# Attention with bias on one core: rests of q loaded earlier, moves of V placed later, a batch closed six outputs from the end, the last exp in two halves

## Chip, cores and metric

The kernel runs on one core of one Trainium2 chip. The metric is device time in microseconds (us) of one execution; lower is better. Five engines work side by side, each through its own list of instructions in order: PE (TensorE, matmuls; PEld is its weight load), ACT (ScalarE), DVE (VectorE), POOL (GpSimd) and SP (SyncE, which here only issues DMAs). Engines wait for one another through semaphores.

## The reference

```python
def reference(q, k, v, bias):            # q, k, v: (4, 8, 1024, 64) f32; bias: (1, 1, 1024, 1024)
    scale = 1.0 / np.sqrt(head_dim)
    scores = scale * np.matmul(q, k.transpose(0, 1, 3, 2))
    scores = scores + bias
    scores_max = np.max(scores, axis=-1, keepdims=True)
    attn = np.exp(scores - scores_max) / (np.sum(np.exp(scores - scores_max), axis=-1, keepdims=True) + 1e-8)
    return np.matmul(attn, v).astype(np.float32)
```

There are 32 heads of 1024 queries, 1024 keys and 64 features; one bias serves all heads.

## The kernel before

**Slots.** Heads come in 16 pairs, queries in 8 chunks of 128. One chunk of one head is a slot, so there are 256 slots. A slot goes through these steps:

- *Fill* (`fill`, L244; 8 matmuls of 128x128): PE writes the scores of 128 queries against 1024 keys into one of three places in PSUM, called 0, 1 and 2 (`places`). A place keeps the score sum of the slot that was there: operands of two neighbouring heads are stacked, one of them negated, so that a fill takes the old head's scores away as it adds the new head's, and the bias stays. A slot that starts a new chunk in a place writes the bias afresh first (L241, 8 more matmuls); slots 0 to 2, 42 to 44, 56, 70 to 72 and seven from 166 on do so. A fill must wait until the exp, or the first DVE step, of the slot that held its place is done.
- *Exp* (`exp`, L258): ACT reads the place and writes the exponentials as bf16, 128x1024 in one instruction. Twenty slots, all of place 2, go to DVE in its place ("DVE slots", `d_steps`): six instructions, of which the first (L275) copies the place out and so frees it, and the others (L280, L284, L287, L290, L295) work out the exponential from that copy, the last writing the bf16 result. No maximum is taken off: the scores are small.
- *Output* (`av`, L312; 8 matmuls): PE multiplies the exponentials with V, which carries a 65th column of ones for the row sum, into a PSUM tile that takes up to seven slots (a batch).
- *Evacuation* (`evac`, L320 and L322): when a batch is closed, DVE takes the reciprocal of the sums and multiplies; then one DMA for each run of neighbouring chunks stores to the output. These are issued on SP, those of the last batches on ACT's queue. The very last output has a tile of its own, `olast`.

**Operands.** K, Q, V and bias are loaded by DMAs that POOL issues in order (L138, L145, L155, L160, L165). K and Q of a pair are transposed on PE (`transposes`, L187 or L191), copied out on DVE (`copy_out`, L199, L201) and doubled into operands for the neighbouring pair (`double`, L210, L212; from pair 7 on by DMAs, L538, after a negated copy, L218). Pairs 0 and 1 load Q in two pieces: three chunks at the start, the other five ("rests", `qrest`) later; the first user of a rest is slot 42. V lands in one of two buffers and is copied by DVE into the wide array `vall` (`move_v`, L492); the load of V of pair p waits for the move of pair p-2.

**Order.** All engines' lists come from a planner written out in the kernel: it keeps an estimated clock for each engine, and always emits the step that could start first. On DVE it picks from `dve_q`, whose entries have an estimated ready time, a priority (0.3 for moves of V, 0.5 for the first step of a DVE slot, 1 for evacuations, 2 for work that is not urgent, 3 and 4 for the later DVE steps) and a cost. Which slots go to DVE is decided when they are filled, from the estimated amount of work that DVE has waiting (`backlog`, `ROOM`) and the number of DVE slots that are open (`open_d`, at most three). ACT takes, of the filled slots, the earliest. The estimates only set the order; on the chip each engine works through its list as the semaphores allow. The early loads are in an order written by hand; `issue` puts a later load on POOL behind a copy (`tick`, L467) that waits for the landing of the load before the last.

Of the kernel before, what the change touches and what calls it, by code (L numbers as in the profile page):

```python
# [16 lines left out]
def kernel(  # L17
# [30 lines left out]
    SPLIT, EARLY = 2, 7  # L48
# [40 lines left out]
    slots = []  # L89
# [20 lines left out]
    NS = len(slots)  # L110
# [10 lines left out]
        at_place[x[0]] = s  # L121

    dslots = set()
    may_d = [x[0] == 2 and 36 < s < NS - 18 and not any(y[3] for y in slots[s:s + 4]) for s, x in enumerate(slots)]

    raws, lands, arrs = {}, {}, {}

# [205 lines left out]
    with tc.manual_schedule():  # L335
# [65 lines left out]
        v_at, vland_at = {}, {0: 13000}  # L401
        t_dma = 15900
        DUE = (64, 82, 94, 106, 117, 126, 134, 142, 150)
        t_pe, t_act, t_dve, t_pool = 9300.0, 9900.0, 9600.0, 9000
        filled, used = {0: T0}, {0: 9900 + L_ACT}
        av_done = {}
# [18 lines left out]
        next_fill, next_act = 1, 1  # L425
        avq = list(range(NS))
        acts = [0]
        dav = []
        dve_q = []
# [7 lines left out]
        sp_q, t_sp = [], T0  # L437
        AHEAD, SLACK = 60, 300
        DEP = 115
        ROOM = 5000  # L440
        MARGIN = 0
        WINDOW = 4

# [46 lines left out]
        def move_v(pr):  # L490
            def run(t2):
                nc.vector.tensor_copy(vall[:, 2 * pr % VR:2 * pr % VR + 2, :, :D], lands[pr, "v"][:])  # L492
                v_at[pr] = t2 + 480 + L_DVE
                next_v(v_at[pr])
            dve_q.append((vland_at[pr], 0.3, 480, run))


        def early(kind, pr):
# [76 lines left out]
        def pe_cands():  # L575

            out = []
            for x in range(3):
                if not queue[x] or queue[x][0] > next_fill + WINDOW:
                    continue  # L580
                s = queue[x][0]
                r = fill_ready(s)
                if r is not None and (before[s] is None or before[s] in used):
                    cost = FILL + BIAS * bool(slots[s][3] and s > 1)

                    def do(t, s=s, x=x, cost=cost):
                        nonlocal next_fill
                        fill(s)
                        filled[s] = t + cost + L_PE
                        queue[x].pop(0)  # L590
                        next_fill = min([y[0] for y in queue.values() if y], default=NS)
                        if may_d[s] and backlog(t) < ROOM and len(open_d) < 3:
                            dslots.add(s)
                            avq.remove(s)
                            start_d(s)
                        else:
                            acts.append(s)
                    out.append((max(t_pe, r), cost, do, 0, s))


            todo = []
            if avq:
                group = [s for s in avq[:1] if round_of[s] == round_of[avq[0]]]
                have = [s for s in group if s in e_at]
                lag = len([s for s in avq[:NE] if s in e_at])
                if len(have) < len(group):
                    group = have if lag >= LAG and have[:1] == avq[:1] else []
                if avq[0] >= NS - 3:
                    group = [s for s in avq[:1] if s in e_at]
                if group and all(slots[s][2] // 2 in v_at for s in group):  # L610
                    todo.append((max(max(e_at[s], v_at[slots[s][2] // 2]) for s in group), group))
            if dav:
                todo.append((dav[0][0], [dav[0][1]]))
            if todo:
                r, group = min(todo)
                b = len(closed)
                if b_tag:
                    tag = b_tag[0]
                    group = group[:7 - len(bank[b][1])]
                else:  # L620
                    f, tag = min((x_free[y], y) for y in x_free)
                    r = max(r, f)
                cost = AVG * len(group) if len(group) > 1 else AV
                if r < 1e11:
                    def do(t, group=group, b=b, tag=tag, cost=cost):
                        b_tag[:] = [tag]
                        x_free[tag] = 1e12
                        av(group, b, tag)
                        for s in group:
                            if s in dslots:  # L630
                                dav.pop(0)
                            else:
                                avq.remove(s)
                            av_done[s] = t + cost
                        next_v(t)
                        n = len(bank[b][1])
                        if n == 7 or n == 6 and not (dav and dav[0][0] < t + cost + 600) or len(av_done) in (NS - 1, NS):
                            closed.append(b)
                            b_tag.clear()
                            close(b, tag, t + cost + L_PE)  # L640
                    out.append((max(t_pe, r), cost, do, 1, 0))
            if pieces:
                pr, which, c0, n = pieces[0]
                need = need_at[pr, which, c0]
                ring = pr + linked(pr) - RING
                lag = len([s for s in avq[:NE] if s in e_at])
                if ((pr, which, c0) in raw_at and next_fill >= need - AHEAD and (ring < 0 or last_slot[ring] < next_fill)
                        and (lag < 4 or need - next_fill < 8)):
                    f, tag = min((x_free[y], y) for y in x_free)
                    r = max(f, raw_at[pr, which, c0])  # L650
                    cost = n * TR + SWITCH * (pr < EARLY or which not in BESIDE)
                    urgent = need - next_fill < 12
                    if r < 1e11:
                        def do(t, pr=pr, which=which, c0=c0, n=n, tag=tag, cost=cost):
                            x_free[tag] = 1e12
                            pieces.pop(0)
                            px = transposes(pr, which, c0, n, tag)
                            if pr < EARLY and which == 0 and c0 == 0:
                                freed(pr, t)

                            def run(t2):
                                copy_out(pr, which, c0, n, px)
                                done = t2 + 60 * n + (180 if which else 300)
                                x_free[tag] = done + L_DVE
                                if which:
                                    ready["ko", pr] = done + L_DVE
                                else:
                                    ready["qo", pr, c0] = done + L_DVE
                                doubles(pr, which, c0, n, done, urgent)
                            dve_q.append((t + cost + L_PE, 0 if urgent else 2, 60 * n + (180 if which else 300), run))  # L670
                        out.append((max(t_pe, r), cost, do, 2 if next_fill < need - 9 else 0.5, 0))
            return out
# [18 lines left out]

        chains, d_wait, open_d = [], [], set()

        def backlog(t):
            x = max(0, t_dve - t) + sum(y[2] for y in dve_q if y[0] < t + 3000 and y[1] < 3)
            return x + sum(sum(y[0] for y in c) for c in chains) / 2 + sum(sum(y[0] for y in c[1:]) for r, s, c in d_wait) / 2

        def start_d(s):
            steps = d_steps(s)
            open_d.add(s)  # L700

            def first(t):
                steps[0][1]()
                used[s] = t + steps[0][0] + L_DVE
                d_wait.append((t + steps[0][0] + DEP, s, steps))
                next_chain(t)
            dve_q.append((filled[s], 0.5, steps[0][0], first))
# [46 lines left out]
            return min(ok + fills, key=lambda x: (x[0], x[3])) if ok + fills else None  # L754

        def dve_pick():
            can = [x for x in dve_q if x[1] < 4 or len(dav) < 2]
            if not can:
                return None
            best = min(can, key=lambda x: (max(x[0], t_dve), x[1]))  # L760
            start = max(best[0], t_dve)

            if best[1] >= 3:
                soon = [x for x in dve_q if x[1] < 3 and x[0] < start + 350]
                if soon:
                    best = min(soon, key=lambda x: (x[0], x[1]))
            return best

        move_v(0)
        for x in ("k3", "q3", "v1", "k4", "q4", "v2", "k5", "q5", "v3", "k6", "q6", "v4", "v5", "b3", "q0", "q1", "b4", "v6", "b5", "b6", "b7"):  # L770
            early(x[0], int(x[1]))
        while next_fill < NS or next_act < len(acts) or avq or dav or dve_q or sp_q:
            c = []
# [21 lines left out]
            t, who = min(c)  # L795
            if who == 0:
                s = acts[next_act]
                exp(s)
                t_act = t + EXP
                next_act += 1  # L800
                used[s] = e_at[s] = t_act + L_ACT
# [41 lines left out]
```

## Time and profile before

| | |
|---|---|
| median of 3 runs | 233.38 us (233.37 to 234.59) |
| the profiled execution's own time | 235.16 us |
| its span (first to last instruction) | 233.4 us |
| granted TensorE clock in it | 0.997 |
| exps on ACT (L258) | 237 instructions, mean 1089 ns of one |
| first DVE steps (L275) | 20, mean 1220 ns |
| moves of V (L492) | 16, median 423 ns |
| loads of the rests of q | 2 of 160 KB as they are stored, median 8.3 us from issue to landing |

An exp's duration includes the time that it waits in ACT's pipeline behind the one before, so the step from one start to the next is the better measure of a busy ACT. The idle time that the profile names stands before an instruction, with what ended it. Idle time of an engine costs something only where another engine comes to wait for it.

### The profile page before, as it was taken

Reading aid. Unit: us, or ns where it says so; the run is one execution under the profiler, and the core shown is the slowest. Engines: PE = TensorE matmul, PEld = TensorE weight load, DVE = VectorE, ACT = ScalarE, POOL = GpSimd, SP = SyncE. Lnnn points to the kernel's source line nnn. Section 1 sums busy time; section 2 is a strip of 40 time slices with the busy share of each in tenths; the row PEclk is TensorE's granted clock in tenths of the full one; section 3 lists DMA queues with packets and bytes.
Section 4 is the critical chain, followed back from the end, with each engine's and each line's share of the span. In section 5 each row is a group of like instructions: output and inputs, shape, how many; then the busy total and the mean of one; then the engine's idle time right before and its main releaser. Section 6 shows DMA issues by size and latency. Waiting matters only on the chain. (4 is left out here: it accounts for less than half of the span.)

```text
span 233.4 us, 10703 instructions
## 1 busy us (share of the span) xinstructions
PE 222.3 (95%) x4671; PEld 209.3 (90%) x4671; DVE 201.5 (86%) x296; ACT 221.1 (95%) x241; POOL 63.4 (27%) x99
## 2 busy tenths in 40 slices
PE   7989999899999999999999997999999999999992
PEld 2869999798999999999999997999999999999982
DVE  2576677599999998999999869999998999999972
ACT  3799999988999999999999998999999999999993
POOL 8943135055446555245352310000000000000000
PEclk9999999999999999999999999999999999999998
DMA  6999979959999899999999992111111111221212
GB/s 206 206 205 215 224 166 158 229 121 150 120 191 137 131 159 183 204 196 157 197 163 201 204 194 68 44 42 39 44 37 42 45 42 42 65 59 42 66 48 56
DMA packets 55646, 29.75 MB, mean 127 GB/s; under 512 B 31472, under 2 KB 51952, under 8 KB 55600
## 3 DMA queue, kind: packets, MB, share of 16 engines
q0 software_dynamic: 30336, 14.06, 48.7%
q1 hardware_dynamic: 24832, 14.40, 22.6%
q8 instruction: 36, 0.59, 1.1%
q10 hardware_dynamic: 432, 0.62, 0.8%
q14 instruction: 10, 0.08, 0.1%
HBM read 29.36 MB, written 8.39 MB: 162 GB/s over the span
## 5 line engine op out<-in xcount | busy, mean ns | idle before, releaser
L258 ACT ACTIVATE E<-pl 128x1024 bf16<-128x1024 f32 (+1 forms) x237 | 218.0, 1089 | 4.3 <-PE pl L244 3.9
L312 PE MATMUL po<-vall,E 128*128 128x65 bf16 x1888 | 93.6, 194 | 0.9 <-ACT E L258 0.9
L312 PEld LDWEIGHTS <-E 128*128 128x128 bf16 x1888 | 78.1, 98 | 1.9 <-ACT E L258 1.2
L244 PE MATMUL pl<-qo,ko 128*128 128x128 bf16 x1024 | 77.3, 219 | 1.7 <-DVE dy L275 1.1
L244 PEld LDWEIGHTS <-ko 128*128 128x128 bf16 x1160 | 69.2, 98 | 4.5 <-issue 1.5
L244 PE MATMUL pl<-qe,ke 128*128 128x128 bf16 x888 | 66.8, 219 | 1.9 <-DVE qe L212 0.5
L244 PEld LDWEIGHTS <-ke 128*128 128x128 bf16 x888 | 53.2, 98 | 5.0 <-issue 1.3
L275 DVE TENSOR_SCALAR dy<-pl 128x1024 int32<-128x1024 f32 x20 | 24.4, 1220 | 2.1 <-PE pl L244 1.4
L322 DVE TENSOR_TENSOR ob<-po,rs 128x448 f32<-128x448 f32 (+2 forms) x39 | 23.2, 594 | 1.9 <-DVE rs L320 0.5
L295 DVE SCALAR_TENSOR_TENSOR de<-dy,dt 128x1024 uint16<-128x1024 int32 x20 | 24.4, 1218 | 0.0
L290 DVE SCALAR_TENSOR_TENSOR dt<-df,dt 128x1024 f32<-128x1024 f32 x20 | 24.4, 1218 | 0.0
L284 DVE SCALAR_TENSOR_TENSOR dt<-df 128x1024 f32<-128x1024 f32 x20 | 24.3, 1217 | 0.0
L287 DVE SCALAR_TENSOR_TENSOR df<-dt,df 128x1024 f32<-128x1024 f32 x20 | 24.3, 1216 | 0.0
L199 DVE COPY ko<-px 128x1024 bf16<-128x1024 bf16 (+1 forms) x16 | 10.7, 671 | 6.9 <-PE px L191 6.3
L165 POOL DMA_DIRECT2D v<-in_v_dram x16 | 11.4, 712 | 18.3 <-DVE vall L492 16.0
L138 POOL DMA_DIRECT2D q<-in_q_dram x18 | 16.0, 890 | 1.3 <-DMA out_dram<-ob 0.5
L201 DVE TENSOR_SCALAR qo<-px,sgn 128x1024 bf16<-128x1024 bf16 (+2 forms) x18 | 12.4, 688 | 4.4 <-PE px L191 3.6
L280 DVE TENSOR_SCALAR df<-dy 128x1024 f32<-128x1024 uint16 x20 | 13.8, 690 | 0.0
L241 PE MATMUL pl<-ident,braw 128*128 128x128 bf16 x136 | 11.5, 228 | 0.1
L145 POOL DMA_DIRECT2D k<-in_k_dram x15 | 11.0, 734 | 2.2 <-PE pl L244 1.0
L320 DVE RECIPROCAL rs<-po 128x7 f32<-128x7 f32 (+3 forms) x40 | 7.8, 195 | 4.4 <-PE po L312 4.0
L467 POOL COPY tick<-q 1x1 bf16<-1x1 bf16 x9 | 3.8, 421 | 24.7 <-DMA q<-in_q_dram 24.7
(54 smaller groups left out, 129.5 us busy)
## 6 DMA issues: line engine op xcount, KB each, us to landing
v<-in_v_dram POOLq DMA_DIRECT2D x16, 256.0 KB, 6.1
k<-in_k_dram POOLq DMA_DIRECT2D x15, 256.0 KB, 5.6
out_dram<-ob SPq DMA_DIRECT2D x32, 96.0 KB, 3.6
out_dram<-ob SPq DMA_DIRECT2D x45, 64.0 KB, 3.2
ke<-ko SPq DMA_DIRECT2D x22, 128.0 KB, 4.9
q<-in_q_dram POOLq DMA_DIRECT2D x18, 128.0 KB, 4.8
qe<-q SPq DMA_DIRECT2D x17, 128.0 KB, 4.9
out_dram<-ob SPq DMA_DIRECT2D x67, 32.0 KB, 1.8
```

The lines of the kernel that those rows point to most:

```text
L138: nc.gpsimd.dma_start(out=t[:, :, y, :], in_=(qf, kf)[x][pr][:, y].rearrange("p (c d) -> p c d", d=D))
L201: nc.vector.tensor_scalar(t["qo"][:, cs, :], px[:], sgn[:], None, op0=ALU.mult)
L244: nc.tensor.matmul(to, kk[:, kc, :], qq[:, c, :], start=False, stop=True, skip_group_check=True)
L258: nc.scalar.activation(e[:, i:i + n].rearrange("p b x -> p (b x)"), places[slots[s][0]][:, i:i + n].rearrange("p b x -> p (b x)"), ACTF.Ex ...
L275: w.tensor_scalar(t["y"][:], places[slots[s][0]].rearrange("p b x -> p (b x)"), scale * LOG2E * 65536.0, 127.0 * 65536.0, op0=ALU.mult, op ...
L280: w.tensor_scalar(t["f"][:], t["lo"], G / 65536.0, None, op0=ALU.mult)
L284: w.scalar_tensor_tensor(t["t"][:], t["f"][:], -G, t["f"][:], op0=ALU.add, op1=ALU.mult)
L287: w.scalar_tensor_tensor(t["f"][:], t["t"][:], Q, t["f"][:], op0=ALU.mult, op1=ALU.add)
L290: w.scalar_tensor_tensor(t["t"][:], t["f"][:], V, t["t"][:], op0=ALU.add, op1=ALU.mult)
L295: w.scalar_tensor_tensor(etile[s].bitcast(U16).rearrange("p c q -> p (c q)"), t["y"][:], 1.0 / 512.0, t["t"][:], op0=ALU.mult, op1=ALU.add)
L312: nc.tensor.matmul(po[:, j + i, :], etile[s][:, kc, :], vall[:, slots[s][2] % VR, kc, :], start=j + i + kc == 0, stop=kc == NCH - 1, skip_ ...
L322: nc.vector.tensor_tensor(ob[:, :n, :], po[:, :n, :D], rs[:, :n, :].to_broadcast([P, n, D]), op=ALU.mult)
```

## The change

The DVE slots are now a list (`PLAN`); it holds the same 20 slots that the rule chose before. Five edits act on the order:

- In the list of early loads, the rests of q of pairs 0 and 1 stand ahead of V of pair 5 and of the bias chunk 3.
- A move of V of pair 7 or later is taken as ready 1500 ns later than its estimated landing.
- A batch is also closed when 250 outputs are done.
- The last exp is issued as two instructions of 512 columns each; the output's matmuls on the first half wait for the first alone.
- A DVE slot counts as open from its first step, and the choice on DVE holds a first step back while three are open; before, the choice of DVE slots did so.

The lists of instructions that come out differ in many places after the early loads: DVE's from its 57th entry on, PE's from the first transpose of a rest on, and the order of the exps from slot 41 on, where the exps of place 2 come one or two later than before.

```diff
-    may_d = [x[0] == 2 and 36 < s < NS - 18 and not any(y[3] for y in slots[s:s + 4]) for s, x in enumerate(slots)]
+    PLAN = (38, 47, 50, 59, 75, 78, 96, 108, 117, 129, 150, 159, 171, 177, 189, 195, 207, 216, 225, 234)
...
-        ROOM = 5000
...
-            dve_q.append((vland_at[pr], 0.3, 480, run))
+            dve_q.append((vland_at[pr] + 1500 * (pr >= EARLY), 0.3, 480, run))
...
-                        if may_d[s] and backlog(t) < ROOM and len(open_d) < 3:
+                        if s in PLAN:
                             dslots.add(s)
                             avq.remove(s)
                             start_d(s)
...
-                        if n == 7 or n == 6 and not (dav and dav[0][0] < t + cost + 600) or len(av_done) in (NS - 1, NS):
+                        if n == 7 or n == 6 and not (dav and dav[0][0] < t + cost + 600) or len(av_done) in (NS - 6, NS - 1, NS):
...
         def start_d(s):
             steps = d_steps(s)
-            open_d.add(s)
-
             def first(t):
+                open_d.add(s)
                 steps[0][1]()
...
         def dve_pick():
-            can = [x for x in dve_q if x[1] < 4 or len(dav) < 2]
+
+            can = [x for x in dve_q if (x[1] < 4 or len(dav) < 2) and (x[1] != 0.5 or len(open_d) < 3)]
...
-                soon = [x for x in dve_q if x[1] < 3 and x[0] < start + 350]
+                soon = [x for x in can if x[1] < 3 and x[0] < start + 350]
...
-        for x in ("k3", "q3", "v1", "k4", "q4", "v2", "k5", "q5", "v3", "k6", "q6", "v4", "v5", "b3", "q0", "q1", "b4", "v6", "b5", "b6", "b7"):
+        for x in ("k3", "q3", "v1", "k4", "q4", "v2", "k5", "q5", "v3", "k6", "q6", "v4", "q0", "q1", "v5", "b3", "b4", "v6", "b5", "b6", "b7"):
...
-                exp(s)
+
+                for i in range(2) if next_act == len(acts) - 1 and next_fill >= NS else (None,):
+                    exp(s) if i is None else exp(s, i, 1)
```

More of the change, by code (lines that the diff above doesn't have):

```diff
@@ L692 @@
         chains, d_wait, open_d = [], [], set()
-        def backlog(t):
-            x = max(0, t_dve - t) + sum(y[2] for y in dve_q if y[0] < t + 3000 and y[1] < 3)
-            return x + sum(sum(y[0] for y in c) for c in chains) / 2 + sum(sum(y[0] for y in c[1:]) for r, s, c in d_wait) / 2
         def start_d(s):
             steps = d_steps(s)
-            open_d.add(s)
             def first(t):
+                open_d.add(s)
                 steps[0][1]()
```

## The prediction

> **What bounds the kernel now.** I read the busy table of the page first.
>
> ```profile
> PE 222.3 (95%) x4671; PEld 209.3 (90%) x4671; DVE 201.5 (86%) x296; ACT 221.1 (95%) x241; POOL 63.4 (27%) x99
> ```
>
> ACT, PE and DVE are all near full, so I ask what one exp costs when nothing holds it up. The chain of waits shows it at the end.
>
> ```profile
> 220.11 0.06 ACT E L258
> 220.17 0.84 issue
> ...
> 227.34 0.16 ACT E L258
> ```
>
> Eight exps start between 220.11 and 227.34: 7.23/8 = 0.904 us from one to the next, although one lasts 1.02 alone. The change keeps the same 20 slots on DVE and 236 on ACT, so that part cannot shrink; only time beyond 0.904 per exp can. The timeline of ACT (idle time before a row in brackets) shows where it is.
>
> ```profile
> 47.53 1.02 ACT L258 ACTIVATE E<-pl 128x1024 bf16<-128x1024 f32 x1 [0.26 <-PE pl L244]
> 48.76 1.02 ACT L258 ACTIVATE E<-pl 128x1024 bf16<-128x1024 f32 x1 [0.21 <-PE pl L244]
> 50.00 4.69 ACT L258 ACTIVATE E<-pl 128x1024 bf16<-128x1024 f32 x5 [0.21 <-PE pl L244]
> 55.28 1.02 ACT L258 ACTIVATE E<-pl 128x1024 bf16<-128x1024 f32 x1 [0.59 <-PE pl L244]
> ...
> 73.14 37.71 ACT L258 ACTIVATE E<-pl 128x1024 bf16<-128x1024 f32 x41 [0.34 <-PE pl L244]
> ...
> 143.24 17.56 ACT L258 ACTIVATE E<-pl 128x1024 bf16<-128x1024 f32 x19 [0.87 <-PE pl L244]
> ```
>
> ACT always waits for a fill. From the exp of slot 39 (44.38) to the last (228.25) there are 197 steps: 183.87 - 197 x 0.904 = 5.8 us lost. By stretch, each counted the same way: 44.38 to 58.91 (14 steps) 1.87; to 74.08 (16) 0.71; to 143.24 (74) 2.26, of which 1.03 in the last step; to 228.25 (93) 0.94. Next, what made PE late, from the timelines of PE and DVE:
>
> ```profile
> 42.11 0.47 PE L191 MATMUL px<-ident,qrest 128*64 128x128 bf16 x10 [0.78 <-DMA qrest<-in_q_dram]
> ...
> 142.59 0.61 PE L244 MATMUL pl<-qo,ko 128*128 128x128 bf16 x8 [1.14 <-DVE dy L275]
> ```
>
> ```profile
> 46.96 0.43 DVE L492 COPY vall<-v 128x1024 bf16<-128x1024 bf16 x1 [0.85 <-DMA v<-in_v_dram]
> ...
> 138.33 0.43 DVE L492 COPY vall<-v 128x1024 bf16<-128x1024 bf16 x1 [1.86 <-DMA v<-in_v_dram]
> ...
> 140.99 0.42 DVE L492 COPY vall<-v 128x1024 bf16<-128x1024 bf16 x1
> 141.32 1.22 DVE L275 TENSOR_SCALAR dy<-pl 128x1024 int32<-128x1024 f32 x1
> ```
>
> One PE stall is the late rest of q; the other is a first DVE step (L275, slot 150), which alone frees place 2, behind two moves of V. The tail, from the SP and ACT timelines:
>
> ```profile
> 225.81 5.35 SPq L688 DMA_DIRECT2D out_dram<-ob  x6
> ...
> 230.53 0.34 ACTq L688 DMA_DIRECT2D out_dram<-olast  x1
> ```
>
> The batch of seven evacuated at 228.91 gives SP five stores at 0.46 each; the last lands at 232.41, after olast (232.25). The span ends 0.98 later.
>
> **Part 1, rests of q ahead of V5.** Today POOL holds both rests behind V5's load, which waits for a V buffer until 32.77; they are issued at 34.05 and land at 42.07 and 43.32. Now they go out at about 27.9 with nothing to wait for, while the q0 queue is nearly empty from 32 to 34, so they land near 35 to 37, well before PE's transposes at about 41.8. No DMA is added. The PE stall goes and the exp of slot 39 starts near 43.9: **-0.48**.
>
> The new DVE order also puts the move of V6 ahead of the copy of q1's rest, its two doubles and slot 38's first step; before, only one double stood behind it. Added wait: DVE comes to it at about 43.5. Behind it on DVE stand 0.43 + 0.56 + 0.33 + 0.33 + 1.22 = 2.9 us to the end of the first step; for that waits PE's fill of slot 41, and behind that fill, in PE's order, all others. PE wants it at about 47.4, so V6 must land by 44.5. It landed at 46.94. Everything in its queue except the rests stays ahead of it; the rests took 42.07 - 38.38 and 43.32 - 42.07, together 4.94 us of the queue. I take that whole: V6 at 42.0, no wait. Ends: 42.0 and (nothing gained) 46.94; two rests at the second one's 1.25 give 44.4, still in time.
>
> The Trainium skill, page "DMA: Bandwidth & Descriptors", section "Anatomy of one DMA — SWDGE (gpsimd) path", fits a POOL-queue DMA as 2.0 us plus bytes over 436 GB/s. By it the two rests (2 x 327,680 bytes) hold the queue only 1.5 us, V6 lands at 45.4 and the sum below would be 0.9 worse. The 4.94 us of this trace speak for more.
>
> Between 44 and 59, what stays: slots 42 and 43 carry bias (16 matmuls, 1.13 us) and now run in two alternating places, since slot 41's comes later. A place that was freed at t gives data at t+1.13+0.05, with one exp (0.904) to cover it: 0.3 to 0.4 lost at each, 0.8 in all, and 0.2 at slot 54, whose fill stands behind slot 50's. So 1.0 for 1.87: **-0.87** (ends 0 and -1.87).
>
> **Part 2, slot order round the DVE slots.** A DVE slot now counts as open from its first step on, not from its fill; that acts only through the order, and the number of evacuations stays 40. The new order takes place 2's exp later, after a DVE slot. At slots 70 and 71 (bias fills, 0.61 lost in one step at 73.14) the order is now 70, 72, 71, so two exps cover each fill: **-0.6** (ends 0, -0.71).
>
> **Part 3, later moves of V.** Moves 7 to 15 stand later on DVE. V14's load waits for V12's move (two buffers) and landed 7.7 us after it; the DVE work between the two moves grows from 5.5 to 6.7 us, so its wait shrinks. Then slot 150's first step follows at once, where before a last step, a copy, a negate and V15's move (1.22+0.74+0.43+0.42 = 2.8) came between; and its successor's exp has one more exp of time. The 1.03 step goes: **-1.03** (ends 0, -1.03). On POOL, K11 and Q11 pass V7, K13 and Q13 pass V9; V9 then lands where Q13 did (106.6), DVE reaches its move near 108. No readers of these V come before it.
>
> **Small stalls.** The remaining 1.23 and 0.94 (alternating places, transposes between two fills) stay: exps that come only two after the last of their place go from 43 to 50. Ends -0.8, +0.8; I take 0.
>
> **Part 4, tail.** Let L be the start of the last exp: today olast is evacuated at L+2.25, the end is L+5.14. The new batch at six from the end takes the five SP stores off the end. But slot 234's last three steps move behind the small batch: its DVE chain starts when slot 248's output is there (L-3.2) and takes 0.75 + 1.14 + 0.55 + 1.14 + 1.22 = 4.8, to L+1.6. The last exp in halves: a half alone took 0.60, a whole 1.02, of which 0.12 hides behind the next one; two halves cost 0.06 to 0.09 more, and let four of eight output matmuls go early (4 x 0.033). So slot 255 is out at L+1.65. Then a batch of five (between 0.46 for two and 0.76 for six: 0.66) to L+2.36, two stores on ACT's queue at 0.42, slot 234 alone (0.43), its store third at L+3.2, landing 1.72 later as olast's did, and 0.98: L+5.9. **+0.8** (ends: 0 if ACT issues faster; +1.8 if DVE comes 1 us late).
>
> **Sum.** -0.48 - 0.87 - 0.6 - 1.03 + 0.8 = -2.2. The profiled execution took 235.16 with a span of 233.4, 1.8 around it; it becomes 233.0. The median of the three runs, 233.38, lies 1.8 below the profiled time; I move it by the same amount: **231.2**.
>
> **Rivals.** (a) *V6 late*: it lands at 45.4 to 46.9, DVE stands 2 to 3 us at the move, fill 41 blocks PE. Cost 0.9 to 2.4: 232.1 to 233.6. For it: DVE waited 0.85 there already. Against: the queue's idle time that the rests now fill. Chance 0.12. (b) *Stalls only move*: the 0.6 and the 1.03 turn up at other transposes and places since PE is nearly full; 232.8. For it: more alternating pairs. Against: DVE now has, up to slot 234's first step, 153.7 us of work against 182 exps, before 155.1 against 179. Chance 0.13. (c) *Slower*: first DVE steps come late. From the exp that frees place 2 to the next exp there: 1.10 + 0.61 + 1.22 + 0.05 + 0.61 + 0.1 = 3.7 us; eleven of the DVE slots leave five exps for it, 4.5 us. If a step of 1.22 already running holds DVE, and it comes over 0.8 late, the rest is lost at each; at 1.1 late on eleven that is 3.3, which makes it slower than before; at 1.22 late with an evacuation of 0.8 before it, 13 us. Against: before had five at nearly every slot and lost 0.94 in the last 85 us. 235.5 as a middle; chance 0.07. (d) *Small stalls go too*, and the tail costs nothing: 231.2 - 0.8 - 0.8 = 229.6; chance 0.1.
>
> **Numbers.** Forecast 0.58 (230.3 to 232.2). With (d), faster by over 0.5% (below 232.2) 0.67; (a), (b): within 0.5% 0.25; slower 0.08. 0.5% is about what a measurement of this kernel tells from no change. Range: from (d) to the dear end of (a), 229.6 to 233.7; out of it lie (c) and the far ends.
>
> **What would show it.** Right: no wait of PE for qrest; V6 landed before 44.5 and no DVE idle time at its move; the exp rows unbroken at 55, 73 and 143; last exp starting near 225.3; olast's store issued about 3.2 after it. Wrong: DVE waiting for v near 43 to 47 with a gap on PE at slot 41; new breaks of ACT over 0.5; a last DVE step after the last exp's end by more than 1 us.

## The result and the profile after

The changed kernel takes 234.93 us (median of 20 runs), the kernel before 233.68 us beside it: ratio 1.0044, 95% interval 1.0024 to 1.0064. It is slower by about 1.0 us; 231.2 was forecast, and 234.93 lies above the range.

The busy table of the changed kernel's page, one line: the engines do the same work as before.

```profile
PE 221.2 (95%) x4671; PEld 209.1 (90%) x4671; DVE 201.2 (86%) x296; ACT 221.0 (95%) x242; POOL 63.2 (27%) x99
```

The timeline of ACT of the changed kernel (start, length, group; in brackets the idle time before it), against the six rows shown of before:

```profile
45.18 1.98 ACT L257 ACTIVATE E<-pl 128x1024 bf16<-128x1024 f32 x2 [0.64 <-PE pl L243]
47.45 1.02 ACT L257 ACTIVATE E<-pl 128x1024 bf16<-128x1024 f32 x1 [0.29 <-PE pl L243]
48.68 25.04 ACT L257 ACTIVATE E<-pl 128x1024 bf16<-128x1024 f32 x27 [0.21 <-PE pl L243]
73.88 37.77 ACT L257 ACTIVATE E<-pl 128x1024 bf16<-128x1024 f32 x41 [0.17 <-PE pl L243]
111.83 116.81 ACT L257 ACTIVATE E<-pl 128x1024 bf16<-128x1024 f32 x128 [0.19 <-PE pl L243]
```

The breaks at 55 and 143 are gone, the one at 73 has shrunk from 0.34 to 0.17, and from 111.83 on ACT's 128 instructions are one row without a break that the timeline shows. What is new is the 0.64 ahead of 45.18: the exp of slot 39 comes 0.8 *later* than before (44.38), where it was to come 0.48 earlier. PE's timeline, and below it the weight loads, say why:

```profile
41.75 0.27 PE L243 MATMUL pl<-qe,ke 128*128 128x128 bf16 x2
42.93 0.49 PE L243 MATMUL pl<-qe,ke 128*128 128x128 bf16 x6 [0.91 <-issue]
43.35 0.47 PE L190 MATMUL px<-ident,qrest 128*64 128x128 bf16 x10
```
```profile
42.93 0.32 PEld L243 LDWEIGHTS <-ke 128*128 128x128 bf16 x5 [1.03 <-issue]
```

The transposes of the rest (L190) wait for no DMA any more: the rests landed at 34.0 and 35.3. But PE stands for a microsecond between the second and the third matmul of one fill, where no semaphore is in play; the profile can only call it "issue".

DVE, at the two places that the forecast named: the move of V6 (L490) and slot 38's first step (L274), then V14's move and slot 150's first step right behind it.

```profile
45.16 0.43 DVE L490 COPY vall<-v 128x1024 bf16<-128x1024 bf16 x1
...
46.80 1.22 DVE L274 TENSOR_SCALAR dy<-pl 128x1024 int32<-128x1024 f32 x1
...
140.48 0.42 DVE L490 COPY vall<-v 128x1024 bf16<-128x1024 bf16 x1
140.82 1.22 DVE L274 TENSOR_SCALAR dy<-pl 128x1024 int32<-128x1024 f32 x1
```

No row has idle time in front: V6 had landed at 44.0, V14 at 139.7. In the tail, from the timelines of DVE and ACT:

```profile
227.72 1.22 DVE L294 SCALAR_TENSOR_TENSOR de<-dy,dt 128x1024 uint16<-128x1024 int32 x1
...
229.87 0.22 DVE L321 TENSOR_TENSOR olast<-po,rs 128x64 f32<-128x64 f32 x1
```
```profile
229.79 0.83 ACTq L686 DMA_DIRECT2D out_dram<-ob  x2
230.72 0.39 ACTq L686 DMA_DIRECT2D out_dram<-olast  x1
```

Slot 234's last step ends after the last exp does (228.64). olast is evacuated at 230.09, but its store goes out only at 230.72, behind two other stores on ACT's queue. From the last exp's end to the end of the span it takes 4.55 (before: 3.84).

**The two profiles side by side mislead.** The spans are 233.19 and 233.39, so the changed kernel looks 0.2 *shorter*, while the medians say 1.25 longer. In every run here the time is the span and 1.8 more. Before's median of 233.68 thus belongs to a span of about 231.9, and the profiled execution of before was one of the longest of its kind. The experiments had to say which of its stalls were the kernel's and which that execution's.

### The profile page after: what moved, and what is told of

It is laid out like the page before. It is cut to its first block, busy times and chain, and to the rows that moved or that the text cites. A ratio compares the mean times of both kernels' runs of the same rounds, so it can differ in the third digit from the quotient of the medians.

```text
span 233.2 us, 10648 instructions
## 1 busy us (share of the span) xinstructions
PE 221.2 (95%) x4671; PEld 209.1 (90%) x4671; DVE 201.2 (86%) x296; ACT 221.0 (95%) x242; POOL 63.2 (27%) x99
## 4 chain that ended last, share of the span: by engine, by line
PE 45%; ACT 35%; issue 9%; DMA 4%; DVE 3%; POOL 3%; DVEq 0%; POOLq 0%
ACT E L257 35%; PE pl L243 26%; PE po L311 13%; DMA q<-in_q_dram 4%; PE px L190 3%; PE pl L240 2%; DVE dy L274 1%; POOL k L144 1%; PE px L186 1%; POOL braw L159 1%; DVE de L294 0%; DVE df L286 0%; DVE dt L289 0%; DVE ob L321 0%; POOL qz L349 0%
## 5 line engine op out<-in xcount | busy, mean ns | idle before, releaser
L311 PE MATMUL po<-vall,E 128*128 128x65 bf16 x1888 | 92.8, 194 | 0.2 <-ACT E L257 0.2
L311 PEld LDWEIGHTS <-E 128*128 128x128 bf16 x1888 | 77.8, 98 | 1.2 <-ACT E L257 0.5
L243 PEld LDWEIGHTS <-ko 128*128 128x128 bf16 x1160 | 69.9, 98 | 6.2 <-issue 2.7
L243 PEld LDWEIGHTS <-ke 128*128 128x128 bf16 x888 | 52.6, 98 | 4.1 <-issue 1.2
L274 DVE TENSOR_SCALAR dy<-pl 128x1024 int32<-128x1024 f32 x20 | 24.4, 1221 | 3.2 <-PE pl L243 3.0
L321 DVE TENSOR_TENSOR ob<-po,rs 128x448 f32<-128x448 f32 (+3 forms) x39 | 23.2, 594 | 1.9 <-DVE rs L319 0.2
L319 DVE RECIPROCAL rs<-po 128x7 f32<-128x7 f32 (+4 forms) x40 | 7.9, 197 | 4.8 <-PE po L311 3.9
L240 PEld LDWEIGHTS <-braw 128*128 128x128 bf16 x136 | 10.0, 148 | 0.1
```

The costliest lines, as they stand in the source:

```text
L240: nc.tensor.matmul(to, braw[:, c, :].rearrange("p (kp kc) -> p kc kp", kc=NCH)[:, kc, :], ident8[:], start=i == 0, stop=False, skip_group_ ...
L243: nc.tensor.matmul(to, kk[:, kc, :], qq[:, c, :], start=False, stop=True, skip_group_check=True)
L274: w.tensor_scalar(t["y"][:], places[slots[s][0]].rearrange("p b x -> p (b x)"), scale * LOG2E * 65536.0, 127.0 * 65536.0, op0=ALU.mult, op ...
L311: nc.tensor.matmul(po[:, j + i, :], etile[s][:, kc, :], vall[:, slots[s][2] % VR, kc, :], start=j + i + kc == 0, stop=kc == NCH - 1, skip_ ...
L321: nc.vector.tensor_tensor(ob[:, :n, :], po[:, :n, :D], rs[:, :n, :].to_broadcast([P, n, D]), op=ALU.mult)
```

## The experiments

Theory A, after the traces: the loss is the stand of PE at 42, because its next block of instructions arrives late (from the packets of queue q8 in the trace), and the tail; the middle gained nothing since an ordinary execution of before has no stall of 1.03 at 143. Rivals: the new order of DVE slots or the later moves cost something; the tail's edits cost; the gap belongs to the fill it stands in.

### Parts of the change

**e1_notail**: the changed kernel without the closing and the halves.

```diff
-  ... or len(av_done) in (NS - 6, NS - 1, NS):
+  ... or len(av_done) in (NS - 1, NS):
-  exp(s) if i is None else exp(s, i, 1)   # for the last exp, in two halves
+  exp(s)
```

> The changed kernel without its two tail edits (no closing at 250 outputs, the last exp whole); all else as in the changed kernel. Theory 1 (the stalls that were priced are smaller in an ordinary execution of the kernel before, and the tail costs 0.7): 234.9 - 0.7, so 234.2, within 0.3% of the kernel before. Theory 2 (the new middle order itself is slower; the tail is free): no change from the changed kernel, 0.4 to 0.5% over the kernel before. Theory 3 (a gap on PE in the middle of one fill near 43 us, 1.0 us long, is the loss and comes back in every execution with the early rests of q): the gap is in this trace too, time 234.2 to 234.9. In all three the last exp starts near 227.4.

Ratio 1.0051 (1.0024 to 1.0078), no better. The end still comes 4.73 after the last exp's end: slot 234 is the last work here too, its last step ending at 229.14, with the last exp's end at 229.12. So the two tail edits are not the loss, and it is not the closing that makes slot 234 late.

**e2_loads** and **e3_moves**: the kernel before with `PLAN` and the later counting of open slots, and either the new order of early loads or the later moves; the planner works out all the rest anew.

> The kernel before with the rests of q ahead of V5 alone (with the list of DVE slots and the count of open slots from their first step, which alone leave the kernel before as it was). Forecast's own pricing: -0.48 at the rests and up to -0.87 to slot 59, so 1.0 faster. Theory 1: 0 to 0.5 faster. Theory 3: the PE gap of 1 us near 43 is in this trace, time 0 to 0.5 slower.

> The kernel before with the later moves of V alone (and the same list and count). Forecast's own pricing: 1.0 faster, no wait of DVE for V14. Theory 1: the wait of DVE for V near 138 is in few executions of the kernel before, so within 0.3 of it. Theory 2: slower by 0.5 to 1.

e2: 1.0092 (1.0058 to 1.0125), slower than the whole change. Its planner put slot 117's first DVE step behind a last step; ACT's timeline of e2:

```profile
117.69 2.85 ACT L258 ACTIVATE E<-pl 128x1024 bf16<-128x1024 f32 x3 [1.73 <-PE pl L244]
```

That is the mechanism of rival (c), at one slot, for 1.7; the changed kernel itself has it nowhere. So e2 says little about the loads (e6 does). e3: 1.0009 (0.9987 to 1.0031), no gain, though DVE no longer waits for V14.

**e4_close**: the kernel before with the closing alone.

```diff
-  ... or len(av_done) in (NS - 1, NS):
+  ... or len(av_done) in (NS - 6, NS - 1, NS):
```

> The kernel before with the closing at 250 outputs alone: four stores go out earlier on SP, the batch after it takes five outputs with slot 234's among them. If the last store of SP set the end, 0.2 faster (olast was 0.16 ahead of it); if the batch of five delays the last evacuation, it is 0.2 to 0.4 slower. Theory 2 has nothing to say of it.

1.0001 (0.9974 to 1.0028). But the end moved: 4.18 after the last exp's end, with three stores ahead of olast's on ACT's queue.

**e11_before_again**: the kernel before, with its DVE slots as a list; instructions and order are the same.

> The kernel before once more (its DVE slots given as the list; the same instructions in the same order). Theory 1: the wait of DVE for V14 (1.86 us in the trace that the forecast read) and the 1.03 us that ACT lost at 143 are not in this execution, nor 0.74 at 55, and its last exp starts 1 to 2 us earlier, near 226.7. If they belong to every execution, they are there again.

233.4 us, span 231.63. Its timelines of ACT and DVE:

```profile
47.27 1.02 ACT L258 ACTIVATE E<-pl 128x1024 bf16<-128x1024 f32 x1 [0.24 <-PE pl L244]
48.49 1.02 ACT L258 ACTIVATE E<-pl 128x1024 bf16<-128x1024 f32 x1 [0.20 <-PE pl L244]
49.72 22.28 ACT L258 ACTIVATE E<-pl 128x1024 bf16<-128x1024 f32 x24 [0.20 <-PE pl L244]
72.34 155.40 ACT L258 ACTIVATE E<-pl 128x1024 bf16<-128x1024 f32 x169 [0.34 <-PE pl L244]
```
```profile
135.96 0.43 DVE L492 COPY vall<-v 128x1024 bf16<-128x1024 bf16 x1 [0.66 <-DMA v<-in_v_dram]
...
139.06 1.22 DVE L275 TENSOR_SCALAR dy<-pl 128x1024 int32<-128x1024 f32 x1
```

PE's timeline of e11, at the transposes of the rest:

```profile
41.49 0.57 PE L191 MATMUL px<-ident,qrest 128*64 128x128 bf16 x10
```

No break at 55, none at 143. DVE waits 0.66 for V14, not 1.86, and slot 150's first step starts at 139.06, not 141.32: early enough that nobody waits. Nor does PE wait for the rest of q: it had landed at 40.88, and PE came to it at 41.49. e4 and e16, whose lists are those of before up to the tail, agree: from the 54th exp to the 191st they take 126.30 and 126.32, as e11 does (126.30), where the profiled before took 127.31. PE's wait for the rest was 0.78 in the profiled before, 0.29 in e16, and none in e11 and e4. The stalls at 47 to 50 and at 72 do recur. So does the end, 3.88 after the last exp (3.84 to 3.88 in five executions with before's tail).

### The loads and PE's instructions

PE's instructions arrive as packets of 16 KB on queue q8 (36 packets, 0.59 MB on the page). In the quiet later part a packet starts within about 1 us of the moment when PE passes the point 64 recorded instructions short of a multiple of 256. Near 40 us it starts later: 3.1 to 3.8 us after that moment with the loads of the kernel before, 3.6 to 5.1 with the rests early, 3.0 to 3.7 where only three loads are under way and 2.5 to 2.6 where only two are. PE can then stand. All 15 stands over 0.2 us that PE's rows call "issue", in eleven of the traces, end 1.2 to 1.6 us after the end of a packet: in the changed kernel the packet ran from 40.38 to 41.45, and PE went on at 42.93. The Trainium skill, page "Runtime: NRT & Kernel Launch", section "Instruction fetch mechanics", describes such a refill in blocks of 256 instructions through a DMA queue and says of it that "ifetch is hidden"; this trace agrees on the blocks, and not on the hiding.

**e8_shifted**: the changed kernel with 24 more matmuls at the start.

```diff
-        for i in range(10):
+        for i in range(9):
...
+        for i in range(25):
+            nc.tensor.matmul(places[2][:, 0, :32], zeros[:, :P], zeros[:, :32], start=True, stop=True)
```

> The changed kernel with 24 matmuls more among the warming ones at the start (one long one replaced by 25 of 32 columns), nothing else. Theory F: the block of instructions ends 48 instructions, that is 24 matmuls, earlier in the work: the gap stands again at the 734th weight load counted from the start, which is now three fills earlier. Theory G: the gap stays in the fill of slot 37, the 758th weight load. Time about that of the changed kernel.

Weight loads of e8 from PE's timeline:

```profile
41.00 0.18 PEld L311 LDWEIGHTS <-E 128*128 128x128 bf16 x3
42.22 0.21 PEld L311 LDWEIGHTS <-E 128*128 128x128 bf16 x5 [1.04 <-issue]
```

The stand is again before the 735th weight load from the start, as in the changed kernel, though that is now an output (L311) some three fills earlier in the program. It goes by the count of instructions, not by what stands there.

**e6_rests_only**: all lists of PE, DVE, ACT and SP as in the kernel before; only POOL issues the rests ahead of V5. (The early loads are written out ahead of the planner's loop, whose estimates stay.)

```diff
+        for x in "k3 q3 v1 k4 q4 v2 k5 q5 v3 k6 q6 v4 q0 q1 v5 b3 b4 v6 b5 b6 b7".split():
...
+            made[...] = loads_of[x[0]](p, *a)
```

> The kernel before with every engine's order kept but POOL's, where the two rests of q go ahead of V5 and of bias chunk 3. The forecast's step on the rests: PE no longer waits for them at 42, 0.5 faster (233.1). Theory F: PE stands at the same place for its instructions instead, the fetch near 40 being later than before: between no change and 0.7 slower (233.6 to 234.3), with a gap in the trace that no DMA of q ends.

0.9994 (0.9962 to 1.0025), no gain. PE's timeline of e6 shows what took the place of the wait for `qrest`, with the rests landed long before:

```profile
42.21 0.41 PE L191 MATMUL px<-ident,qrest 128*64 128x128 bf16 x8 [1.03 <-issue]
```

**e5_paced**, **e7_rests_paced**, **e9_three**, **e10_rests_three**: the loads of the changed kernel (e5, e9) or of e6 (e7, e10) held back, so that only two or three are under way.

```diff
+            if x in ('v5', 'b3', 'b4', 'v6', 'b5', 'b6', 'b7'):      # e5, e7: two under way
+                nc.gpsimd.tensor_copy(tick[:], last[-2])
+            if x in ('b3', 'b4', 'v6', 'b5', 'b6', 'b7'):            # e9, e10: three under way
+                nc.gpsimd.tensor_copy(tick[:], last[-3])
```

> The changed kernel with every engine's order kept, but POOL paces the early loads from V5 on: each first waits (a one-element copy) for the landing of the load before the last, so at most two are under way. Theory F (PE runs out of instructions: its next block of 256, a 16 KB transfer on the instruction queue, starts 3.5 to 5 us late behind a full load queue, where 0 to 0.7 is usual in the quiet part; PE stands where more than about 3.5 us are lost): the fetch near 40 starts under 3 us late, the gap in the middle of the fill near 43 is gone, 0.7 to 1.2 faster than the changed kernel, so about 233.9. Theory G (the gap is something of that fill, not of the fetch): gap and time stay, 234.9.

> As the kernel before this one, with the early loads from V5 on paced by POOL as in the paced changed kernel. Theory F: neither the rests nor the instructions are late, 0.4 to 0.9 faster than the kernel before (232.7 to 233.2). Theory G: as without pacing.

> The changed kernel, every order kept, the early loads from bias chunk 3 on paced with three under way in place of two. Theory F: V6 lands at about 44 as in the changed kernel (no wait of DVE over 0.5 at its move), and the instruction fetch near 40 starts 3 to 3.7 us late in place of 4.2 to 5.1: the gap in the fill near 43 is under 0.4; 0.4 to 0.8 faster than the changed kernel, 234.1 to 234.5 where that is 234.9. If the fetch is held up by the transfers already running alone and not by those queued, the gap stays at 1 us and so does the time.

> The kernel before with the rests of q early, and the early loads from bias chunk 3 on paced with three under way; all other orders kept. Theory F: neither wait is left at 42, 0.3 to 0.8 faster than the kernel before. Otherwise within 0.3 of it.

e5: 1.0156 (1.0101 to 1.0210); e7: 1.0129 (1.0075 to 1.0183). The packet of e5 started at 38.88 and the stand in the fill went, but V6 landed at 47.1. From DVE's and PE's timelines of e5:

```profile
47.13 0.43 DVE L490 COPY vall<-v 128x1024 bf16<-128x1024 bf16 x1 [2.98 <-DMA v<-in_v_dram]
...
48.74 1.23 DVE L274 TENSOR_SCALAR dy<-pl 128x1024 int32<-128x1024 f32 x1
```
```profile
50.02 0.61 PE L243 MATMUL pl<-qo,ko 128*128 128x128 bf16 x8 [1.92 <-DVE dy L274]
```

This is rival (a) in full, brought about by the pacing: DVE at the move, the first step behind it, PE's fill blocked, and a break of 1.7 on ACT, within the 0.9 to 2.4 that it was priced at. (The medians of e5 and e7 lost more, 3 to 4.5; their profiles, at the low end of their runs, don't show where the rest went.)

e9: packet at 39.03, no stand, V6 landed at 43.7, exp of slot 39 at 44.16; the last exp ended 0.67 earlier than in the changed kernel. The median, 234.38, was also lower than the changed kernel's 234.93, but the ratio to its own runs of before was 1.0047 (1.0024 to 1.0069): by ratio no gain is shown. e10: 1.0017 (0.9993 to 1.0041), no gain where 0.3 to 0.8 us was expected; a stand of 0.31 is left at 41.86.

### The tail

**e12_tail_order**: e9 with other priorities for the DVE steps of slots 225 and 234.

```diff
-            dve_q.append((t, 3 if len(left) > 1 else 4, cost, run))
+            dve_q.append((t, 3 if s == 234 else 0.6 if s == 225 else 3 if len(left) > 1 else 4, cost, run))
```

> The kernel of e9_three with one more edit that acts from slot 216 on: every step of slot 225 after the first gets priority 0.6 and every one of slot 234 gets 3, so that the last step of slot 234 is listed on DVE before the last exp and not after it, and the last output of all is that of slot 255 and no longer that of slot 234. Up to about 205 us all lists are those of e9_three. Theory (the tail's loss comes from slot 234 being the last work, not from the closing at six from the end or the halves): the last DVE step ends before the last exp does, the end comes 3.9 to 4.2 after the end of the last exp (4.55 in the changed kernel, 3.84 in the one before), so 0.4 to 0.6 less than e9_three, a median near 233.9 and a ratio of 1.001 to 1.003 to the kernel before. Rival (DVE has too much left in the last 10 us, whatever the order): slot 216's last step takes the place of slot 234's, an evacuation or an output comes late instead, and the end stays at 4.5 or more after the last exp; ratio 1.004 to 1.006.

1.0044 (1.0018 to 1.0070): the theory was wrong by half. From DVE's and ACT's timelines of e12:

```profile
225.98 1.22 DVE L295 SCALAR_TENSOR_TENSOR de<-dy,dt 128x1024 uint16<-128x1024 int32 x1
...
228.55 0.23 DVE L322 TENSOR_TENSOR olast<-po,rs 128x64 f32<-128x64 f32 x1
```
```profile
228.47 1.80 ACTq L687 DMA_DIRECT2D out_dram<-ob  x4
230.37 0.39 ACTq L687 DMA_DIRECT2D out_dram<-olast  x1
```

The last step now ends before the last exp (227.67), and olast is evacuated 1.11 after it in place of 1.45. But the batch of five, no longer of neighbouring chunks, needs four stores, all on ACT's queue ahead of olast's, and the end comes 5.17 after the last exp. Theory B: the stores ahead of olast's are a cost of their own.

**e13_after_again, e14_stores_split, e15_three_split, e16_close_split**, on one chip, one after the other: the changed kernel unaltered; with the stores of the last batch but one shared by SP and ACT; the same with e9's loads; and the kernel before with e4's closing and the shared stores.

```diff
-                for to, of_ in evac(b):
-                    w = nc.scalar if last else nc.sync
+                for i, (to, of_) in enumerate(evac(b)):
+                    w = nc.scalar if last and (i % 2 or len(units) == 1) else nc.sync
```

> The changed kernel once more, unaltered, as the reference for the three kernels beside it. Theory: PE stands about 1 us in the fill of slot 37 again, the end comes 4.5 to 4.6 after the end of the last exp, ratio to the kernel before 1.003 to 1.006. Rival (its profile, too, was an execution out of the ordinary): a gap under 0.5 or an end 0.3 nearer.

> The changed kernel, with the two stores of the last batch but one split: the first on SP, the second on ACT's queue (before, both on ACT's queue, ahead of the store of olast). All other lists are as they were. Theory (0.6 of the tail is olast's store waiting behind two stores on ACT's queue: in the changed kernel olast was evacuated at 230.09 and its store issued at 230.72): olast's store goes out within 0.2 of its evacuation, the end comes 4.0 to 4.1 after the last exp's end in place of 4.55, ratio 0.002 under e13_after_again's. Rival (the end is set by the landing of the batch's stores or by slot 234's last DVE step alone): end still 4.4 to 4.6 after the exp, no difference to e13_after_again.

> The kernel of e9_three (three early loads under way) with the stores split as in e14_stores_split. Theory (fetch gap and tail are the two losses): no gap in slot 37's fill, last exp 0.6 to 0.7 earlier than in e13_after_again, end 4.0 to 4.1 after the last exp's end; ratio 1.000 to 1.002, some 0.005 under e13_after_again's. Rival (the gap costs nothing in the median, PE makes it up later): the same as e14_stores_split.

> The kernel before with the closing at six from the end (as e4_close) and the three stores of that last batch but one split, two on SP and one on ACT's queue. In e4_close olast was evacuated at 228.96 and its store issued at 229.79, behind three stores on ACT's queue. Theory (the closing was worth something and the stores ahead of olast's took it back): olast's store goes out within 0.2 of its evacuation, the end comes 3.4 to 3.6 after the last exp's end (3.84 in the kernel before, 4.2 in e4_close), ratio 0.997 to 0.999: faster than both kernels, though by little. Rival (the landing of the stores on SP ends the span): 3.8 or more, ratio 1.000.

| | ratio to before | end after the last exp's end |
|---|---|---|
| e13, changed kernel | 1.0039 (1.0013 to 1.0064) | 4.55 |
| e14, stores shared | 1.0024 (1.0005 to 1.0044) | 4.16 |
| e15, and three loads under way | 1.0007 (0.9986 to 1.0028) | 4.18 |
| e16, before, closing, stores shared | 0.9967 (0.9948 to 0.9986) | 3.54 |

PE's timeline of e13, then ACT's of e14 and of e16:

```profile
43.49 0.49 PE L243 MATMUL pl<-qe,ke 128*128 128x128 bf16 x6 [1.62 <-issue]
```
```profile
229.79 0.36 ACTq L686 DMA_DIRECT2D out_dram<-ob  x1
230.25 0.39 ACTq L686 DMA_DIRECT2D out_dram<-olast  x1
```
```profile
228.41 0.36 ACTq L688 DMA_DIRECT2D out_dram<-ob  x1
229.03 0.34 ACTq L688 DMA_DIRECT2D out_dram<-olast  x1
```

The stand is there again, 1.62. In e14 olast's store goes out 0.16 after its evacuation, and the end is 0.39 nearer, as theory B had it; the medians of the two don't show it (e13 234.46, e14 234.61). In e16 the end is 0.64 nearer than in e4, and 0.3 nearer than in the kernel before: **e16 is faster than both kernels**, the only one of the runs that is. The step from e14 to e15 is 0.87 in the medians (234.61, 233.74), what the gap was to give, but the intervals of the ratios overlap: that the stand costs its full microsecond in the median is likely and not shown. For the stand and the shared stores together it is: e15's runs are shorter than e13's by 0.8 us in the mean (233.98 and 234.77; 95% interval 0.1 to 1.5). e15 has a stand of its own at another block, which its profile calls the same:

```profile
125.17 0.34 PE L243 MATMUL pl<-qe,ke 128*128 128x128 bf16 x3 [0.65 <-issue]
```

The packet ahead of it ended at 123.92.

**e17_moves_split**: e3 with the shared stores, for the moves' own worth.

> The kernel of e3_moves (the kernel before with the later moves of V; that order closes batch 38 with six slots) with the three stores of the last batch but one split as in e16_close_split; in e3_moves the store of olast went out at 229.13, 0.92 after its evacuation, behind three stores on ACT's queue, and the end came 4.66 after the last exp's end. Theory (the later moves are worth some 0.5 in the stretch of exps, and e3_moves lost that in its tail): the last exp ends near 227.2 to 227.5, the end comes 3.5 to 3.8 later, ratio 0.994 to 0.998. Rival (the earlier last exp of e3_moves was a lucky execution, the moves are worth nothing): the last exp ends at 227.7 or later, ratio 0.998 to 1.001.

1.0005 (0.9980 to 1.0031), last exp's end at 227.95: the rival was right. From the exp of slot 39 to the last exp it took 182.36, in e3 182.35, in e11 182.31. The moves are worth nothing.

## Why the prediction was wrong

The terms, each against both executions of before, from the starts of the exps of the same number (the 40th is slot 39's):

| stretch | forecast | against the profiled before | against e11, near the median |
|---|---|---|---|
| to the 40th exp (rests of q) | -0.48 | 45.18 - 44.38 = +0.80 | 45.18 - 44.13 = +1.05 |
| 40th to 54th | -0.87 | 13.75 - 14.53 = -0.78 | 13.75 - 13.98 = -0.23 |
| 54th to 191st (slots 70 and 71, slot 150) | -1.63 | 126.38 - 127.31 = -0.93 | 126.38 - 126.30 = +0.08 |
| 191st to the last exp's end | 0 | 43.33 - 43.32 = 0.0 | 43.33 - 43.33 = 0.0 |
| tail | +0.8 | 4.55 - 3.84 = +0.71 | 4.55 - 3.88 = +0.67 |
| sum | -2.2 | -0.2 | +1.6 |

Each column compares two single executions; the medians differ by 1.25.

1. **Moving the sum to the median failed.** The prediction read its stalls off one execution, which was 1.8 us over the median, and took the whole sum off the median, as if the median had the same stalls. But those 1.8 us were the stalls: the span was 233.39 against 231.63 in e11. The 1.03 at 143 and most of the break at 55 belong to that execution; e11, e4 and e16 don't have them. The change does remove them (-0.78 - 0.93 = -1.71 in the third column), but the median hardly had them: -0.15 in the fourth. This is the larger failure: 1.6 of the 3.7 between 231.2 and 234.93; another 0.8 is that the forecast for these two stretches (-2.5) was too high even for the profiled execution.

2. **The rests of q: the step that put -0.48 on PE's wait failed**, by 1.3 against the profiled execution and by 1.5 against e11. The rests came as early as forecast. But this wait, too, was hardly in the median: e11 and e4 have none. And in the profiled execution the rest was only the releaser that came last. PE's instruction packet had ended at 40.47; going on 1.2 to 1.6 after it, as in the 15 stands, PE would have been held until about 41.7 to 42.0 in any case, and the rest ended the wait at 42.07. So at most 0.4 could be won there. What was lost is new: with the rests early the load queue holds more, the packet came at 40.38 in place of 39.52, and PE stood longer than before. The exp of slot 39 started at 45.17 to 45.74 in four executions with these loads (the changed kernel, e13, e14, e1), at 43.63 to 44.38 in six with before's (the profiled one, e11, e4, e16, e3, e17), and at 43.63 to 44.16 in three with the rests early and three loads under way (e9, e12, e15). e6 shows that the wait for the rest is replaced by a stand and nothing is won, e8 that the count of instructions decides where PE stands, e9 and e15 that fewer loads under way bring the packet earlier (39.0 and 38.7) and the stand away.

3. **V6** was right in what counted: landed by 44.5, no wait. By the row it was to land at 42.0, by the fit of the Trainium skill, page "DMA: Bandwidth & Descriptors", section "Anatomy of one DMA — SWDGE (gpsimd) path", at 45.4; it landed at 44.0. The 4.94 us that the prediction took for two rests were thus not the price of the two alone: issued early, the second landed 1.26 after the first, the spacing by which the prediction's other bound was 44.4.

4. **44 to 59**: what was to stay did. Bias fills of slots 42 and 43 lost 0.41 and 0.33 (0.3 to 0.4 each forecast), slot 54's 0.25 (0.2). What was to go was only partly there in an ordinary execution.

5. **Slots 70 to 72**: 0.42 lost in two steps in place of 0.61; about 0.1 was forecast. **Slot 150**: no wait for V14, its first step right behind the move, no break, all as told, and worth nothing in the median, which had no break there. The **small stalls** moved, and came to 0.3 more between the 54th exp and the 191st, where zero was taken; that is inside the ends of 0.8 either way. V9 landed at 102.2, not 106.6, and was moved at 112.2, not 108; nothing waited for it.

6. **The tail** was sized right, partly by luck: olast's store at 3.27 after the last exp's start (3.2 forecast), +0.7 in all. But the prediction put slot 234's late steps down to the small batch ahead of them, and e1 has them as late without that batch. Which part of the new order makes slot 234 late is not separated: in e2 and e3, with one part each, its last step ends over 2 us before the last exp does. The parts of the tail, from the profiles: the closing brings the end 0.34 nearer where its stores are out of the way (e16 against e11, 3.54 for 3.88); stores ahead of olast's take 0.39 in the changed kernel (e14) and 0.64 in e4; slot 234 as the last work, with the halves, takes 4.16 - 3.54 = 0.62. The prediction had the two stores on ACT's queue as a stage of the sum and not as a price that could be saved. The halves were not run alone.

Of the rivals, (b), stalls only move, is nearest: what was lost at slots 70 and 71 came back in part there and in part elsewhere, and the 1.03 was not in the median to begin with. (a) and (c) did not happen in the changed kernel; e5 and e2 show that both exist. The price of (a) fits e5's profile and not its median, and (c) took 1.7 at one slot, where the dearest case was 13 us on eleven. The case on the slower side that did happen, PE waiting for its own instructions, was not among the rivals.

## What to carry to other kernels

Hold the profiled execution against the median before summing its stalls, and look for a second execution of the same lists: a stall that only one of them has can't be won in the median. When a wait is removed, ask what else ended at about the same time. Where PE, 95% busy, stood in the middle of a run of equal matmuls and the profile named "issue", its instructions were late each time here; a deeper load queue made that worse, while a shallower one made data late (two under way cost about 3 us and more, three nothing measurable). In a tail, count the issues ahead of the last store on its queue: sharing two or three stores with a second queue brought the end of the span 0.4 to 0.6 us nearer in the profiles. In the times it shows where it was added to the closing alone (e16, 0.9967 of before); none of the reordering showed a gain.

## What the runs showed of the hardware

Not expected: PE's instructions arrive by DMA in packets of 16 KB. Near 40 us, among the loads, a packet starts 2.5 to 5.1 us after PE has come to the point of a block at which, in a quiet stretch, packets start within about 1 us. PE went on 1.2 to 1.6 us after the packet's end in all 15 stands, which were 0.2 to 1.6 us long. Why the packet waits so long is open: its own transfer took 0.9 to 1.8 us.

Also not expected: the end of this program is very repeatable, 3.84 to 3.88 after the last exp in five executions of before's tail and 4.53 to 4.57 in five of the changed one's, so a change of the tail could be read from one profile here, while the stretch of loads up to 45 us moved by up to 0.7 us between executions of the same lists (the exp of slot 39 at 43.63 in e3 and at 44.32 in e17, whose lists differ in the tail alone).
